# A hybrid RWKV and attention block on one core: other tiles' work on VectorE queued behind the inverse, chunk-local products in pairs of groups

## The chip, the core and the metric

The kernel runs on one core of a Trainium2 chip. A core has five engines with instruction queues of their own: TensorE (matmuls; PE in the profile, PEld its weight loads), VectorE (DVE), ScalarE (ACT), GpSimd (POOL) and SyncE (SP, here only a queue of DMA issues). Each works through its queue in order and waits for semaphores of the others. The metric is the device time of one execution, in microseconds; lower is better.

## The reference

One layer over 512 positions of width 2048, batch 1, all in float32. The RWKV branch and the attention branch share one normalised input, and their gated sum goes through an output projection.

```python
def hybrid_layer(x, ...):
    h = rms_norm(x, norm_g)
    proj = jnp.einsum('btd,de->bte', h, w_in)
    shifted = centred_shift(proj[..., :SHIFT_WIDTH], shift_mu)
    xr, xk, xv, wdown, adown = _split(shifted, SHIFT_SIZES)
    z_r, q, k, v, z_a, gates = _split(proj[..., SHIFT_WIDTH:], REST_SIZES)
    o_r = rwkv7_bidir(xr, xk, xv, wdown, adown, ...) * jax.nn.silu(z_r)
    o_a = axial_gqa(q, k, v, q_norm_g, k_norm_g) * jax.nn.silu(z_a)
    p_r = jnp.einsum('btc,cd->btd', o_r, w_branch_rwkv)
    p_a = jnp.einsum('btc,cd->btd', o_a, w_branch_attn)
    merged = sigmoid(g_r) * p_r + sigmoid(g_a) * p_a
    return x + jnp.einsum('btd,de->bte', merged, w_out)

def _wkv_step(S, inp):          # rwkv7_bidir scans this over time, in both directions
    w, kk, b, k, v, r = inp
    sa = jnp.einsum('dbhvk,dbhk->dbhv', S, -kk)
    S = S * w[..., None, :] + sa[..., None] * b[..., None, :] + v[..., :, None] * k[..., None, :]
    return S, jnp.einsum('dbhvk,dbhk->dbhv', S, r)
```

`rwkv7_bidir` has 16 heads of 64 channels. Behind the scan come a group norm over each head's channels, scale and bias, and a term `coef * v`. A final RMS norm ends the reference.

## The kernel before, in words

Every large product is split in a high and a low float32r part, and is made as three matmuls of 128x512 ("dense" work, line 291, tile `acc`). The weights come in quarter strips (`raw` by DMA on SP, high part `wh` on ACT, low part `wl` on DVE, line 265; twelve matmuls each).

The RWKV branch is worked in eight tiles of 128 channels (two heads), each in chunks of 64 positions. A tile passes through these steps:

- `stage_a(i)`: rates and decays. It loads `la` (SP, 1 MB), maps it (L504, DVE), normalises `kk` (`pss`, `rs`, `rb`, `prb`), and for both directions makes a running sum (L517, a scan on DVE; L522 its correction), exponentials (ACT, L530 to L532), and the products `BK` (L538, DVE) with help from POOL. Temporaries come from a ring `temp` of four buffers.
- `tile_task(i)`: products `AL` (DVE, L556 to L559), then chunk-local products `lr` (L571, TensorE) in four visits, each of one group of two chunks; each visit writes two PSUM banks, which DVE (L574 to L578) and ACT (L573) empty. Then `pv`, and the inverse of the chunks' triangular matrices on DVE: 30 steps of L607 and L608, and transposes and copies that end with L625 (`XB`). On TensorE the transposes `tb` (L633) and a product `pcf` (L637, L638) follow the `lr` visits. Flag `B` is set there; the task then waits `subwait`, 50000 ns of the planner's time, and goes on with `pq` (L645) and `px` (L653), which need the inverse.
- The chain over chunks, eight times: `pa` (L678), ACT copies `a0s` and others (L680 to L683), `pu` (L693), ACT copies, `px2` (L700), and the new state `SV` on DVE (L706, four pieces), which the next `pa` needs. POOL prepares `SV` and `sd` (L673, L689).
- `stage_e(i)`: group norm (L722 to L730 on DVE, a square on ACT, a power on POOL), transposes `pg` (L736), two products (L742, L743), and a store to DRAM on POOL's queue. `sz` is loaded on SP's queue.

PSUM has eight banks: two for `acc`, a ring of three named "g" (`g_tile`) and a ring of three named "c" (`c_tile`, used by the chain).

The order on TensorE in this part is the order in which the program issues it. `Weave` is a planner at build time: tasks are generators which yield (cost, wait, flag needed), in ns; while no task is due, it issues one dense matmul and counts `UNIT` for it. The order on the other engines is worked out by the scheduler of the tile framework from its own estimated times. Strips `k`, `r` and `v` of a tile wait for flag B of the tile before. The rest of the input projection (60 strips) fills in. Behind the RWKV part come the attention stage (64 units, with what is left of the input strips, and then the products of the RWKV branch from `oq` as filler; there TensorE's order too is the scheduler's), the products of the attention branch, and the output projection.

Of the kernel before, what the change touches and what calls it, by code (L numbers as in the profile page):

```python
# [100 lines left out]
class Weave:  # L101
# [3 lines left out]

    UNIT = 217
    LAG = 100
# [105 lines left out]

OPT = dict(manual=True, tls=True, sub="dve", subwait=50000, fwait=6000, gn=15000, u1=0, u2=0, c1=700, c2=700, c3=1150, fly=3, scale='pool', prb=4, low=1300, warm=24, rwt='tile', every=2, auto=1, man=1)

# [9 lines left out]
def emit_all(nc, tc, A, out, dbg):  # L225
# [252 lines left out]

    fact = {}

    def stage_a(i):
# [21 lines left out]
        ve.tensor_copy(rb, rs[:, 8:16].rearrange("p (t h) -> p t h", h=2).unsqueeze(3).to_broadcast([128, 4, 2, C]))  # L503
        ve.tensor_scalar(out=la, in0=la, scalar1=0.5, scalar2=0.5, op0=ALU.mult, op1=ALU.add)  # L504
        yield 250, 4500, None
        prb = g_tile("prb")
        for tt in range(4):
            pe.transpose(prb[:, tt * 128:(tt + 1) * 128], rb[:, tt].rearrange("p h c -> p (h c)"), ident)
        ve.tensor_tensor(out=kk, in0=kk, in1=prb, op=ALU.mult)
        ks = rw.tile([128, T], F32, name="ks", bufs=2)  # L510
        dirs = []
# [31 lines left out]
        W.flag(f"A{i}", 6000)  # L543
        yield 428, 0, None

    def tile_task(i):
# [16 lines left out]
        for c in range(0, NC, 2):  # L563
            two = slice(c, c + 2)

            lr = [g_tile("lr").rearrange("p (d c t) -> p d c t", d=2, c=2) for _ in range(2)]
            for d in range(2):
                for j in range(2):
                    for eo in range(2):
                        h0 = 64 * eo  # L570
                        pe.matmul(lr[eo][:, d, j, :], lhsT=BK[h0:h0 + 64, d, c + j, :], rhs=AL[h0:h0 + 64, d, c + j, eo, :], start=True, stop=True)  # L571
            m2 = lambda rows, eo, c0_, c1_: mk[rows, :, eo, c0_:c1_].unsqueeze(2).to_broadcast([64, 2, 2, c1_ - c0_])
            ac.copy(LB[lo_, :, two, :], lr[0][lo_, :, :, 0:C])  # L573
            ve.tensor_tensor(out=AL[hi_, :, two, 0, :], in0=lr[0][hi_], in1=m2(hi_, 0, 0, 128), op=ALU.mult)  # L574
            ve.tensor_tensor(out=L2[lo_, :, two, 0, C:128], in0=lr[0][lo_, :, :, C:128], in1=m2(lo_, 0, C, 128), op=ALU.mult)
            ac.copy(LB[hi_, :, two, :], lr[1][hi_, :, :, C:128])
            ve.tensor_tensor(out=AL[lo_, :, two, 1, :], in0=lr[1][lo_], in1=m2(lo_, 1, 0, 128), op=ALU.mult)
            ve.tensor_tensor(out=L2[hi_, :, two, 1, 0:C], in0=lr[1][hi_, :, :, 0:C], in1=m2(hi_, 1, 0, C), op=ALU.mult)  # L578
            yield 900, 2300, None
        pv = g_tile("pv")  # L580
# [42 lines left out]
        for q in range(4):  # L623
            rows = slice(q * 32, q * 32 + 32)
            ve.tensor_copy(XB[rows], XT[1 - q % 2][rows, 1 - q % 2])  # L625
            for d in range(2):
                ac.copy(XP[rows, d, :, q * 32:(q + 1) * 32], XT[d][rows, d])

        for d in range(2):
            for g in range(2):  # L630
                tb = g_tile("tb").rearrange("p (c h t) -> p c h t", c=4, h=2)
                for j in range(4):
# [6 lines left out]
        ve.tensor_tensor(out=ks, in0=pcf, in1=v, op=ALU.mult)  # L639
        W.flag(f"B{i}")  # L640
        yield 432, OPT['subwait'], None

# [19 lines left out]
        for n in range(NC):  # L662
# [22 lines left out]
            if n < NC - 1:  # L685
                for d in range(2):
                    for eo in range(2):
                        h = slice(64 * eo, 64 * eo + 64)
                        po.tensor_scalar(out=sd[h, d, eo, :], in0=SV[h, d, eo, 0, :], scalar1=PC[h, d, cc[d]:cc[d] + 1], scalar2=0.0, op0=ALU.mult, op1=ALU.add)  # L689
            yield 450, OPT['c1'], None  # L690
            pu = c_tile("pu").rearrange("p (d x) -> p d x", d=8)
# [20 lines left out]
        ve.tensor_tensor(out=O[:, 0], in0=O[:, 0], in1=O[:, 1], op=ALU.add)  # L712
        ow = ch(temp("ow"))
        ve.tensor_tensor(out=ow, in0=O[:, 0, 0:NC, :], in1=O[:, 0, NC:2 * NC, :], op=ALU.add)
        W.flag(f"D{i}")
        W.add(2, stage_e(i, ow, ks))
        yield 450, 0, None

    def stage_e(i, ow, ks):

        s8 = rw.tile([128, 32], F32, name="s8")
        ve.tensor_reduce(out=s8[:, 0:8], in_=ow, axis=AX.X, op=ALU.add)  # L722
        ve.tensor_scalar(out=s8[:, 8:16], in0=s8[:, 0:8], scalar1=-1.0 / C, scalar2=None, op0=ALU.mult)
# [6 lines left out]
        ve.tensor_tensor(out=ow, in0=ow, in1=s8[:, 24:32].unsqueeze(2).to_broadcast([128, NC, C]), op=ALU.mult)  # L730
        gc = temp("gc")
        yield 0, OPT['gn'], None
        for g in range(2):
            pg = g_tile("pg").rearrange("p (c e t) -> p c e t", c=4, e=2)
            for j in range(4):
                pe.transpose(pg[0:64, j].rearrange("p e t -> p (e t)"), ow[:, 4 * g + j, :], ident)  # L736
            for eo, h0 in ((1, 0), (0, 64)):
                ac.copy(ch(gc)[h0:h0 + 64, 4 * g:4 * g + 4, :], pg[0:64, :, eo, :])
            yield 428, 0, None
        sz = rw.tile([128, T], F32, name="sz", tag="sz")  # L740
        sp.dma_start(out=sz, in_=fsp[i])
        ve.scalar_tensor_tensor(out=gc, in0=gc, scalar=pc(P_GW + i), in1=ks, op0=ALU.mult, op1=ALU.add)  # L742
        ve.scalar_tensor_tensor(out=gc, in0=gc, scalar=pc(P_GB + i), in1=sz, op0=ALU.add, op1=ALU.mult)  # L743
        po.dma_start(out=osp[i], in_=gc)
        tap(f"og{i}", gc)

    W.flag("ad", 4500)
# [344 lines left out]
```

## Time and the profile before

| What | us |
|---|---|
| median of 3 runs | 1792.86 (1791.39 to 1794.54) |
| the profiled execution's own time | 1792.16 |
| its span | 1789.9 |
| TensorE busy | 1717.1 (96%) |
| DVE busy | 1221.1 (68%) |
| ACT busy | 812.6 (45%) |
| POOL busy | 554.0 (31%) |

The time of an execution is a little longer than the span from its first to its last instruction. Busy time counts an engine's instructions from start to end. A wait is put down to the engine whose semaphore came last. The granted clock is that of TensorE, as a share of 2.4 GHz.

### The profile page before, as it was taken

Reading aid. Unit: us, or ns where it says so; the run is one execution under the profiler, and the core shown is the slowest. Engines: PE = TensorE matmul, PEld = TensorE weight load, DVE = VectorE, ACT = ScalarE, POOL = GpSimd, SP = SyncE. Lnnn points to the kernel's source line nnn. Section 1 sums busy time; section 2 is a strip of 40 time slices with the busy share of each in tenths; the row PEclk is TensorE's granted clock in tenths of the full one; section 3 lists DMA queues with packets and bytes.
Section 4 is the critical chain, followed back from the end, with each engine's and each line's share of the span. In section 5 each row is a group of like instructions: output and inputs, shape, how many; then the busy total and the mean of one; then the engine's idle time right before and its main releaser. Section 6 shows DMA issues by size and latency. Waiting matters only on the chain. (4 is left out here: it accounts for less than half of the span.)

```text
span 1789.9 us, 26075 instructions
## 1 busy us (share of the span) xinstructions
PE 1717.1 (96%) x8972; PEld 1431.3 (80%) x8972; DVE 1221.1 (68%) x2360; ACT 812.6 (45%) x1827; POOL 554.0 (31%) x824
## 2 busy tenths in 40 slices
PE   6999999999999999999999999999989998999997
PEld 6877887887887887887887888888768886788876
DVE  6577859759959948967957957923788887443342
ACT  5544354354354444344344344344566666232231
POOL 3131062053153143053053043022555554331110
PEclk9999999999999999999999999999999999999999
DMA  6564323423323322423323322433443320435452
GB/s 219 167 201 122 106 63 111 108 60 98 103 77 104 104 63 92 111 74 100 106 77 95 105 67 82 116 89 108 149 149 104 99 92 26 143 108 154 130 171 106
DMA packets 96851, 194.87 MB, mean 109 GB/s; under 512 B 11088, under 2 KB 11344, under 8 KB 95312
## 3 DMA queue, kind: packets, MB, share of 16 engines
q1 hardware_dynamic: 77616, 152.18, 29.7%
q10 hardware_dynamic: 15264, 28.46, 4.4%
q0 software_dynamic: 3840, 12.59, 2.4%
q8 instruction: 71, 1.16, 0.3%
q14 instruction: 60, 0.49, 0.1%
HBM read 162.77 MB, written 30.41 MB: 108 GB/s over the span
## 5 line engine op out<-in xcount | busy, mean ns | idle before, releaser
L291 PE MATMUL acc<-hh,wl 128*128 128x512 f32 (+1 forms) x1388 | 552.1, 398 | 5.1 <-DVE wl L265 5.1
L291 PE MATMUL acc<-hh,wh 128*128 128x512 f32 (+1 forms) x1388 | 554.2, 399 | 0.6 <-ACT wh L264 0.6
L291 PE MATMUL acc<-hl,wh 128*128 128x512 f32 (+1 forms) x1388 | 551.3, 397 | 2.8 <-DVE hl L386 2.2
L265 DVE TENSOR_TENSOR wl<-raw,wh 128x512 fp32r<-128x512 f32 x445 | 331.9, 748 | 278.7 <-ACT wh L264 268.3
L264 ACT CAST wh<-raw 128x512 fp32r<-128x512 f32 x472 | 292.3, 620 | 499.9 <-PE acc L291 348.3
L291 PEld LDWEIGHTS acc<-hh,wl 128*128 128x128 f32 x1388 | 263.2, 190 | 57.5 <-DVE wl L265 8.2
L291 PEld LDWEIGHTS acc<-hl,wh 128*128 128x128 f32 x1388 | 263.4, 190 | 53.1 <-DVE hl L386 4.2
L291 PEld LDWEIGHTS acc<-hh,wh 128*128 128x128 f32 x1388 | 263.4, 190 | 51.5 <-ACT wh L264 1.7
L673 POOL TENSOR_SCALAR SV<-VT 64x128 f32<-64x128 f32 x256 | 82.2, 321 | 214.3 <-PE px L700 110.1
L706 DVE SCALAR_TENSOR_TENSOR SV<-px,PC,sd 64x64 f32<-64x64 f32 x224 | 63.5, 283 | 79.6 <-PE px L700 73.3
L689 POOL TENSOR_SCALAR sd<-SV,PC 64x64 f32<-64x64 f32 x224 | 89.5, 400 | 17.4
L291 PE MATMUL acc<-oq,wh 128*128 128x512 f32 x256 | 84.1, 400 | 4.0 <-ACT oq L946 4.0
L607 DVE TENSOR_TENSOR tm<-B 128x30 f32<-128x30 f32 (+14 forms) x240 | 82.3, 343 | 6.1
L608 DVE TENSOR_TENSOR B<-B,tm 128x30 f32<-128x30 f32 (+14 forms) x240 | 81.1, 338 | 6.0
L527 POOL TENSOR_TENSOR ks<-ks,k 128x512 f32<-128x512 f32 x8 | 15.2, 1901 | 223.4 <-ACT wh L264 84.0
L1023 PE MATMUL of<-wl,mh 128*128 128x512 f32 x192 | 75.0, 391 | 1.8 <-DVE wl L265 1.8
L678 PEld LDWEIGHTS pa<-SV,AL 128*128 128x128 f32 x512 | 67.3, 191 | 10.2 <-POOL SV L673 2.3
L1024 PE MATMUL of<-wh,ml 128*128 128x512 f32 x192 | 74.7, 389 | 0.0
L700 PEld LDWEIGHTS px<-SV,L 128*128 128x128 f32 x512 | 67.9, 193 | 7.3 <-ACT SV L694 1.8
L678 PE MATMUL pa<-SV,AL 128*128 128x64 f32 x512 | 67.2, 271 | 3.3 <-DVE SV L706 3.3
L1022 PE MATMUL of<-wh,mh 128*128 128x512 f32 x192 | 66.1, 389 | 0.0
L700 PE MATMUL px<-SV,L 128*128 128x64 f32 x512 | 65.6, 271 | 0.0
(688 smaller groups left out, 2879.4 us busy)
## 6 DMA issues: line engine op xcount, KB each, us to landing
raw<-in_w_in_dram SPq DMA_DIRECT2D x344, 256.0 KB, 3.1
raw<-in_wo_dram SPq DMA_DIRECT2D x64, 256.0 KB, 2.8
fsp<-tg ACTq DMA_DIRECT2D x60, 256.0 KB, 2.5
tsp<-la ACTq DMA_DIRECT2D x32, 256.0 KB, 3.4
la<-tsp SPq DMA_DIRECT2D x8, 1024.0 KB, 5.0
raw<-in_wbr_dram SPq DMA_DIRECT2D x32, 256.0 KB, 3.1
tgm<-fsp POOLq DMA_DIRECT2D x32, 256.0 KB, 3.5
raw<-in_wba_dram SPq DMA_DIRECT2D x32, 256.0 KB, 2.9
```

The costliest lines, as they stand in the source:

```text
L264: ac.copy(dst_hi, src)
L265: (eng or ve).tensor_tensor(out=dst_lo, in0=src, in1=f(dst_hi), op=ALU.subtract)
L291: pe.matmul(acc[:, tok], lhsT=w[1 if u == 2 else 0][:, j, :], rhs=(xl if u == 1 else xh)[:, kt, tok], start=(kt == 0 and u == 0 and tok.st ...
L607: se.tensor_tensor(out=tv, in0=B[:, 0:s, s:s + 1].to_broadcast([128, s, n]), in1=B[:, s:s + 1, s + 1:32].to_broadcast([128, s, n]), op=ALU ...
L608: se.tensor_tensor(out=B[:, 0:s, s + 1:32], in0=B[:, 0:s, s + 1:32], in1=tv, op=ALU.add)
L673: po.tensor_scalar(out=SV[v0:v0 + 64, d, eo], in0=src.unsqueeze(1).to_broadcast([64, 2, C]), scalar1=1.0, scalar2=0.0, op0=ALU.mult, op1=A ...
L678: pe.matmul(pa[:, d, eo, :], lhsT=AL[:, d, cc[d], eo, :], rhs=SV[:, d, eo, 0, :], start=True, stop=True)
L689: po.tensor_scalar(out=sd[h, d, eo, :], in0=SV[h, d, eo, 0, :], scalar1=PC[h, d, cc[d]:cc[d] + 1], scalar2=0.0, op0=ALU.mult, op1=ALU.add)
L700: pe.matmul(px2[:, d, eo, :], lhsT=L2[:, d, cc[d], eo, :], rhs=SV[:, d, eo, 1, :], start=True, stop=True)
L1022: pe.matmul(acc, lhsT=mh[:, dt, tok(tt)], rhs=w[0], start=(dt == 0), stop=False)
L1023: pe.matmul(acc, lhsT=mh[:, dt, tok(tt)], rhs=w[1], start=False, stop=False)
L1024: pe.matmul(acc, lhsT=ml[:, dt, tok(tt)], rhs=w[0], start=False, stop=(dt == NKT - 1))
```

## The change

`UNIT` goes from 217 to 227 and `subwait` from 50000 to 45500. A helper `behind(i)` puts the instructions of a block, on their engine, behind the last copy of tile i's inverse. The mapping of `la` in `stage_a(i)` is put behind the inverse of tile i-1, and the first group norm instruction of tile i behind the inverse of tile i+1, for which the task also waits for a flag X, set 3000 ns before `subwait` ends. `stage_a` from the third tile on waits for the end of an older tile's group norm (flag E) before it takes `ks`; the output `ow` has a buffer of its own, `sz` takes one of the ring, and its load is issued before `pg`. The `lr` products go two groups a visit, one of the two banks of a group from each ring; `tb` alternates between the rings. The first chunk waits 1600 ns longer between `pa` and `pu`.

```diff
-    UNIT = 217
+    UNIT = 227
-OPT = dict(... subwait=50000, ...)
+OPT = dict(... subwait=45500, ...)
+    fact, inv = {}, {}
+    def behind(i):
+        return tc.issue_after(inv[i].ins) if i in inv else nullcontext()
 def stage_a(i):
-        ve.tensor_scalar(out=la, in0=la, scalar1=0.5, scalar2=0.5, op0=ALU.mult, op1=ALU.add)
+        with behind(i - 1):
+            ve.tensor_scalar(out=la, in0=la, scalar1=0.5, scalar2=0.5, op0=ALU.mult, op1=ALU.add)
...
         ve.tensor_tensor(out=kk, in0=kk, in1=prb, op=ALU.mult)
+        if i >= 2:
+            yield 428, 0, f"E{i - 2}"
...
-        yield 428, 0, None
+        yield 0 if i >= 2 else 428, 0, None
 def tile_task(i):
-            lr = [g_tile("lr").rearrange(...) for _ in range(2)]
+            lr = [t_("lr").rearrange(...) for t_ in (g_tile, c_tile)]
...
-            yield 900, 2300, None
+            if c == 2:
+                yield 1800, 5000, None
+        yield 1800, 3000, None
...
-            ve.tensor_copy(XB[rows], XT[1 - q % 2][rows, 1 - q % 2])
+            inv[i] = ve.tensor_copy(XB[rows], XT[1 - q % 2][rows, 1 - q % 2])
...
-                tb = g_tile("tb").rearrange(...)
+                tb = (g_tile if g else c_tile)("tb").rearrange(...)
...
         W.flag(f"B{i}")
+        W.flag(f"X{i}", OPT['subwait'] - 3000)
...
-            yield 450, OPT['c1'], None
+            yield 450, OPT['c1'] + (1600 if n == 0 else 0), None
...
-        ow = ch(temp("ow"))
+        if i:
+            yield 450, 0, f"E{i - 1}"
+        ow = ch(rw.tile([128, T], F32, name="ow", tag="ow"))
...
-        yield 450, 0, None
+        yield 0 if i else 450, 0, None
 def stage_e(i, ow, ks):
+        if i < NT - 1:
+            yield 0, 0, f"X{i + 1}"
-        ve.tensor_reduce(out=s8[:, 0:8], in_=ow, axis=AX.X, op=ALU.add)
+        with behind(i + 1):
+            ve.tensor_reduce(out=s8[:, 0:8], in_=ow, axis=AX.X, op=ALU.add)
...
-        gc = temp("gc")
         yield 0, OPT['gn'], None
+        gc, sz = temp("gc"), temp("sz")
+        sp.dma_start(out=sz, in_=fsp[i])
         for g in range(2):
...
-            yield 428, 0, None
-        sz = rw.tile([128, T], F32, name="sz", tag="sz")
-        sp.dma_start(out=sz, in_=fsp[i])
...
         po.dma_start(out=osp[i], in_=gc)
+        W.flag(f"E{i}")
+        yield 856, 0, None
```

## Rows read from the trace of the kernel before

**Rows 1.** The page, busy time: us, share of the span, instructions.

```profile
PE 1717.1 (96%) x8972; PEld 1431.3 (80%) x8972; DVE 1221.1 (68%) x2360; ACT 812.6 (45%) x1827; POOL 554.0 (31%) x824
```

**Rows 2.** Waits of TensorE, 140 to 1250: waited for, total, times, longest.

```profile
PE lr L571 <- DVE s L728: 9.6, 3, 3.7
PE pu L693 <- ACT a0s L681: 5.8, 10, 3.1
PE lr L571 <- DVE L L575: 4.4, 3, 2.1
PE tb L633 <- ACT VT L584: 3.6, 5, 0.7
PE pa L678 <- DVE SV L706: 3.3, 5, 1.9
```

**Rows 3.** Timeline of TensorE, third tile, second `lr` visit: start, length, what.

```profile
421.76 1.13 PE L571 MATMUL lr<-AL,BK 64*128 64x128 f32 x14 [2.97 <-DVE s L728]
...
423.83 0.63 PE L291 MATMUL acc<-hh,wl 128*128 128x512 f32 x1
424.26 0.63 PE L291 MATMUL acc<-hh,wh 128*128 128x512 f32 x1
```

**Rows 4.** Timeline of DVE, the same stretch.

```profile
413.30 1.22 DVE L504 TENSOR_SCALAR la<-la 128x2048 f32<-128x2048 f32 x1
414.44 0.68 DVE L722 TENSOR_REDUCE s<-ow 128x8 f32<-128x512 f32 x1
...
415.63 1.22 DVE L517 TENSOR_TENSOR_SCAN cs<-con,la 128x512 f32<-128x512 f32 x1
...
417.49 0.69 DVE L724 TENSOR_TENSOR ow<-ow,s 128x512 f32<-128x512 f32 x1
...
420.49 0.69 DVE L574 TENSOR_TENSOR AL<-lr,con 64x512 f32<-64x512 f32 x1
```

**Rows 5.** Timeline of TensorE around one undisturbed `lr` visit.

```profile
287.39 0.39 PE L291 MATMUL acc<-hl,wh 128*128 128x512 f32 x1
287.71 1.16 PE L571 MATMUL lr<-AL,BK 64*128 64x128 f32 x16
288.80 0.50 PE L291 MATMUL acc<-hh,wl 128*128 128x512 f32 x1
289.14 0.39 PE L291 MATMUL acc<-hh,wh 128*128 128x512 f32 x1
289.37 0.40 PE L291 MATMUL acc<-hl,wh 128*128 128x512 f32 x1
```

**Rows 6.** Stretches: length, busy us of each engine, granted clock, DMA.

```profile
420.00:440.00 20.00, 17.47 (x109) 14.13 (x110) 16.27 (x33) 10.63 (x23) 6.25 (x12) 0.91 0.28 80
635.00:655.00 20.00, 16.95 (x89) 14.67 (x88) 7.63 (x16) 9.91 (x31) 5.23 (x16) 0.83 0.22 63
695.00:715.00 20.00, 17.23 (x102) 13.87 (x103) 15.24 (x30) 9.08 (x21) 5.42 (x9) 0.83 0.26 79
...
1515.00:1540.00 25.00, 20.17 (x69) 15.29 (x70) 10.37 (x16) 6.79 (x12) 10.43 (x11) 0.80 0.39 124
```

**Rows 7.** Timelines of DVE and TensorE, fourth tile: the inverse ends, `pq` starts.

```profile
617.28 0.59 DVE L625 COPY XX<-RR 32x256 f32<-32x256 f32 x2
...
628.43 0.42 PE L645 MATMUL pq<-XX,LQ 128*128 128x32 f32 x3
```

**Rows 8.** Stretches behind the second tile's inverse; columns PE, PEld, DVE, ACT, POOL.

```profile
343.00:357.00 14.00, 14.00 (x70) 11.82 (x68) 7.26 (x13) 4.97 (x9) 0.09 (x1) 1.00 0.43 104
356.00:375.00 19.00, 17.74 (x116) 15.26 (x115) 15.96 (x21) 10.50 (x29) 13.24 (x12) 1.00 0.19 55
```

**Rows 9.** Line L538 on DVE: ns min/median/max, first and last start.

```profile
L538 DVE TENSOR_TENSOR BK<-ke,la x16: 683/1664/1782, 113.8 to 1046.8; 64x512 f32<-64x512 f32 x16
```

**Rows 10.** Waits of TensorE, 1250 to 1530.

```profile
PE acc L291 <- ACT oq L946: 4.0, 1, 4.0
PE acc L291 <- ACT oah L264: 3.4, 1, 3.4
PE acc L291 <- DVE tgm L988: 2.3, 1, 2.3
```

More of the change, by code (lines that the diff above doesn't have):

```diff
@@ L211, in step @@
         return True
-OPT = dict(manual=True, tls=True, sub="dve", subwait=50000, fwait=6000, gn=15000, u1=0, u2=0, c1=700, c2=700, c3=1150, fly=3, scale='pool', prb=4, low=1300, warm=24, rwt='tile', every=2, auto=1, man=1)
+OPT = dict(manual=True, tls=True, sub="dve", subwait=45500, fwait=6000, gn=15000, u1=0, u2=0, c1=700, c2=700, c3=1150, fly=3, scale='pool', prb=4, low=1300, warm=24, rwt='tile', every=2, auto=1, man=1)
 def context(nc):
@@ L477, in filler @@
         strip(s, done)
-    fact = {}
+    fact, inv = {}, {}
+    def behind(i):
+        return tc.issue_after(inv[i].ins) if i in inv else nullcontext()
     def stage_a(i):
@@ L564, in tile_task @@
             two = slice(c, c + 2)
-            lr = [g_tile("lr").rearrange("p (d c t) -> p d c t", d=2, c=2) for _ in range(2)]
+            lr = [t_("lr").rearrange("p (d c t) -> p d c t", d=2, c=2) for t_ in (g_tile, c_tile)]
             for d in range(2):
@@ L630, in tile_task @@
             for g in range(2):
-                tb = g_tile("tb").rearrange("p (c h t) -> p c h t", c=4, h=2)
+                tb = (g_tile if g else c_tile)("tb").rearrange("p (c h t) -> p c h t", c=4, h=2)
                 for j in range(4):
```

## The prediction

> **What bounds the kernel now.** I read the share of busy time first. TensorE is busy for 1717.1 us of a span of 1789.9 [rows 1], so the end is set by the matmul queue, and a gain can come only from the 73 us in which that queue stands still, from the time in which it runs at a lower granted clock, and from gaps between matmuls. The second view is therefore the list of TensorE's waits between 140 and 1250 us, where the eight RWKV tiles are worked [rows 2]. The chunk-local products `lr` (L571) wait 9.6 us for DVE's L728 and 4.4 us for DVE's L575; the transposes `tb` (L633) wait 3.6 us; `pu` (L693) waits 5.8 us for ACT's `a0s`; `pa` (L678) waits 3.3 us for DVE's `SV`. None of these is a wait for data of the weights. L728 is group norm of the tile before, and has nothing to do with `lr`.
>
> The third view, the timelines of both engines, shows why. The third tile's second `lr` visit stops after two matmuls and stands 2.97 us [rows 3]. It needs the PSUM bank of the first visit, and DVE empties that bank only from 420.49 us on [rows 4], because the rates of the next tile (1.22 us), its scan (1.22), and group norm (0.68 and 0.69 shown, two like them and two small ones not shown) stand ahead of it in DVE's queue. After the stall the dense matmuls come 0.43 us apart [rows 3] and not 0.23 [rows 5]: the granted clock has fallen to the lower of its two levels, 1.2 GHz. The fourth view gives that a price: mean granted clock by stretch [rows 6]. A mean of 0.91 over 20 us is 1.8 us of lost matmul time, 0.83 is 3.4, and 0.80 over 25 us is 5.0.
>
> The planner's fill is not lost when a wait is shortened. Dense matmuls that no longer stand inside a tile are issued later, so I count stalls, clock and gaps, and not the shorter waits themselves.
>
> **What the change removes from `lr`.** The pieces of rows 4 that stand ahead of the bank's emptying are all queued behind a tile's inverse, and the two `lr` banks now come from two rings of three, so that a visit of two groups takes four banks of six. The second visit begins 23 dense matmuls later (5000/227, rounded up), 23 x 0.23 = 5.3 us; its second group alone reuses banks, and reaches them after its first group, 1.09 us [rows 5], 6.4 us after the first visit. Emptying one group costs DVE about 2.2 us (0.69 for one of two large pieces in rows 4, and two of half the columns), so it is done in time even with two weight pieces of 0.68 between. The 14.0 us of `lr` waits in rows 2 go. `tb` wants a bank right behind `pv`; its first bank now comes from the other ring and has been free for a visit, so the 3.6 us go as well. Sum 17.6; bounds 0 to 17.6; I take 17, since the timelines name the pieces one by one.
>
> **Fewer visits.** Into a visit the step is 0.32 us where dense matmuls are 0.23 apart, out of it 0.34 [rows 5]: 0.09 + 0.11 = 0.2 us a visit. Two visits instead of four, eight tiles: 16 x 0.2 = 3.2 us. Nothing in the rows excludes that as small a gap appears elsewhere: bounds 0 to 3.2, I take 3.2.
>
> **The shorter wait for the inverse** (`subwait`, and `UNIT`). Before it is 50000/217, 231 dense matmuls; after it is 45500/227, 201. That is 30 x 0.23 = 6.9 us earlier for `pq`. The inverse of the fourth tile ends at 617.87 us and `pq` starts at 628.43 [rows 7]: 10.6 us of slack, of which 3.7 stay. So the cost is nothing, hidden under dense work; if the inverse came later by more than 3.7 us, each us more would be one us for each of eight tiles. It should not come later: what is now emptied in two groups (4.4 us) was before held up by group norm.
>
> **What is moved, and where it lands.** Rates, first scan, and group norm now start when the inverse ends, some 4 us ahead of `pq`. In that stretch today DVE is busy 7.26 of 14 us and POOL 0.09 [rows 8]. The moved pieces by rows 4 are 1.22 + 1.22 + four of 0.69 or so, 4 us, plus the correction of the scan (0.7) and the products with `gc` (2 us): about 6.7 us. They don't fit whole into the 3.7 us that are left. Behind it lies the stretch 356 to 375, in which DVE is already busy 15.96 of 19 us [rows 8] with the products `BK`, and the chain over chunks starts there: each chunk needs a `SV` product from DVE (four pieces, 1.2 us together) with only six dense matmuls, 1.4 us, to cover it. What is queued behind DVE's `SV` is `pa` of the next chunk on TensorE's queue, in order, and all dense work behind that. So the saturated stretch grows from two chunks to about four. Today `pa` loses 3.3 us [rows 2] over some 14 such chunks, 0.24 each; 28 of them at the same rate lose 6.7, and I take 7.3, a cost of 4 us. Bounds: a gain of 3.3 (if the order within DVE falls well) and a loss of 43 (28 times 1.66, the median of the slow `BK` pieces of rows 9, less today's 3.3).
>
> What could make the moved pieces dearer is POOL. One kind of `BK` product takes 683 ns at best and 1664 in the median, in one shape [rows 9], and in the stretch 356 to 375 POOL is busy 13.24 of 19 us [rows 8]. If the four moved pieces with two inputs slip past `pq` and stretch as these do, each costs 1.0 us more (1.66 - 0.69); ahead of `pq`, where POOL idles, nothing. The Trainium skill, "SBUF — State Buffer", section "Who interferes with whom", says that a VectorE instruction with two SBUF inputs contends with a GpSimd instruction that reads SBUF, and that one blocks the other for the whole instruction; the trace's two durations agree. By that rule 4 us of DVE a tile are at risk and by the row of the idle stretch none; it is the mechanism of the first rival below.
>
> The other moves. The load of `sz` (SP) and the store of `gc` (POOL) go with group norm; SP's queue stands ahead of TensorE by three quarter strips of weights, and the waits of rows 2 name no weight piece, so both cost nothing; if that cover were gone, a load would show as `acc` waiting for `wl`. Waits for E (a tile's group norm ended) before `ks` and `ow`: by the planner's constants the group norm of the tile before ends 42.5 + 15 us behind the B mark, and the chain only starts at 45.5, with eight chunks to go, so nothing waits. What these waits hold up is a task of the planner, not an engine.
>
> **`pu` of the first chunk** has 1600 ns more cover, 7 dense matmuls, 1.6 us. Of the 5.8 us in rows 2 the longest was 3.1, which it halves; ACT gets exponentials of the moved scan there too. I take a gain of 4 (bounds 0 and 5.8).
>
> **The clock.** The dips at 420 and 695 us (1.8 and 3.4) follow `lr` stalls and go with them; the one at 635 (3.4) follows the longest `pu` wait. That is 8.6; I put one dip of 1.8 back for the longer `SV` waits: gain 6.8, bounds 0 and 8.6.
>
> **The attention stage.** Per tile the planner places fewer dense matmuls: 30 (`subwait`), 7 (`lr`: 44 before, 37 after), one before `lr`, less 7 (first chunk): 31 x 8 = 248, 57 us of work that moves behind the eighth tile. Today the attention stage runs out of such work: TensorE waits 3.4 us for the last head and 2.3 for a gate at its end [rows 10], and loses 5.0 to the clock there [rows 6]. With 57 us more in hand these 10.7 can be covered. But the wait for `oq`, 4.0 us [rows 10], which follows the last `w_in` strip, moves into the middle of attention and may grow. Bounds: gain 10.7, loss 4; I take a gain of 7.
>
> **The sum**, against the profiled execution's own 1792.2 us (0.7 below the median of the runs, a difference I neglect): -17 - 3.2 - 4 + 4 - 6.8 - 7 = -34.0, so 1758 us.
>
> **Rivals.** (1) The moved pieces slip past `pq` and stretch beside POOL, 4 us of DVE a tile, so the crowding is worse than today's rate: each of the 28 `SV` pieces is 0.6 us late, 17 us instead of 7.3, with three more dips of 1.8: 10 + 5.4 = 15 us back, 1773. For it: DVE has 3 us free in 19 already. Against: today's 0.24. (2) The other side: each `SV` waits behind one whole `BK` piece of 1.66 us, 46 us, 43 more than today, and every tile but the last has a dip, 10.8 beyond the one counted. Without its 4 us for `SV` the sum is -38; -38 + 43 + 10.8 = +16, 1808. The point from which it decides is (38 - 10.8 + 3.3)/28, about 1.1 us of lateness per `SV`. Against: the queue's order is written down beforehand from estimated durations, and today's order loses a quarter of that. (3) The inverse is late for `pq`: 6 us later than today is 2.3 us on eight tiles, 18 us, with a dip each 14: 32 back, 1790, no change. For it: a remaining slack of 3.7 us. Against: what was ahead of it is taken away.
>
> **How the numbers follow.** The forecast, with 1743 (every bound in favour: 17.6 + 3.2 + 5.8 + 3.3 + 8.6 + 10.7 = 49.2) to 1768 as its own range, 0.62. Rival 1, 0.20. Rival 2, 0.09. Rival 3, 0.05. The remaining 0.04 is below 1743: short waits and dips that the rows shown leave out. The range of 8 in 10 reaches from 1739 to 1784. A measurement of this kernel tells 0.2% from no change. Faster by more than that, 0.85; within, 0.06; slower, 0.09.
>
> **What would show it.** Right: in the list of TensorE's waits `lr` and `tb` all but vanish; a tile has two `lr` visits of 32; DVE's L504, L722 and L724 stand behind L625; dense work from `oq` is left after the last head, and the dips at 420, 635 and 695 have no successors. Wrong: `pa` waiting for L706 far beyond 7 us, `pq` waiting for L622, `acc` waiting for `wl`, or a new wait of `pg` for group norm.

## The result, and the profile after

The changed kernel takes 1802.50 us (median of 7 runs, 1797.59 to 1808.81), the kernel before 1791.39 beside it on the same chip (1789.84 to 1794.54). The ratio is 1.0062, 95% interval 1.0040 to 1.0083: slower by 0.6%, where 1.9% faster was forecast. The span of the profiled execution is 1802.9 us, 13.0 more than before.

The busy times of the page after, to be held beside [rows 1]:

```profile
PE 1730.0 (96%) x8972; PEld 1454.1 (81%) x8972; DVE 1209.8 (67%) x2358; ACT 813.4 (45%) x1827; POOL 572.3 (32%) x826
```

TensorE has as many instructions as before and is busy 12.9 us longer. That is all but 0.1 us of the longer span; so the time in which TensorE stands still is the same in sum, and it has only changed its place. Two stretches by windows say where, of the kernel before and then of the one after (length, busy time of PE, PEld, DVE, ACT, POOL, granted clock, DMA share, GB/s):

```profile
140.00:1200.00 1060.00, 1030.08 (x5621) 862.63 (x5621) 799.80 (x1595) 468.80 (x1156) 310.12 (x569) 0.99 0.33 93
1200.00:1600.00 400.00, 385.55 (x1984) 321.37 (x1983) 267.33 (x527) 212.31 (x436) 184.57 (x201) 0.98 0.36 110
```

```profile
140.00:1200.00 1060.00, 1017.66 (x5520) 861.46 (x5519) 786.37 (x1599) 463.37 (x1171) 330.29 (x595) 0.95 0.30 87
1200.00:1600.00 400.00, 394.54 (x2011) 330.43 (x2010) 262.78 (x512) 210.71 (x406) 177.29 (x173) 1.00 0.39 119
```

In the RWKV part TensorE stood still for 1060 - 1030.1 = 29.9 us and now for 42.3, and the granted clock fell from 0.99 to 0.95. In the attention part it stood still for 14.5 and now for 5.5, and the clock rose to 1.00. The second row is the gain that was forecast there; the first is the loss. Its waits by name, TensorE between 140 and 1250 us of the kernel after (total, times, longest):

```profile
PE pa L688 <- DVE SV L716: 16.2, 11, 3.0
PE px L710 <- ACT SV L704: 12.0, 5, 2.5
PE pu L703 <- ACT a0s L691: 5.8, 8, 1.1
PE px L663 <- ACT LQ L659: 5.5, 4, 2.8
PE pss L502 <- ACT sq L497: 2.5, 1, 2.5
```

Against [rows 2], every wait of `lr` and `tb` is gone, as forecast. In their place stand the links of the chain over chunks: `pa` for the state `SV`, 16.2 us for 3.3, and two waits that were not in the list before, of both products named `px` for ACT's copies, 17.5 together. (L688, L703 and L710 are L678, L693 and L700 of the code shown above, L663 is L653, and L659 makes its `LQ`; L545 below is L538, L716 is L706, L704 and L705 are the copies of `pu` into `SV`, L513 is `prb`.)

What such a wait looks like: the fifth tile's chain, third and fourth chunk. First TensorE, then ACT, then DVE of the kernel after (start, length, what, idle time before it and its releaser):

```profile
764.14 0.66 PE L703 MATMUL pu<-a0s,XP 128*128 128x64 f32 x4 [0.91 <-ACT a0s L691]
...
768.14 1.97 PE L710 MATMUL px<-SV,L 128*128 128x64 f32 x8 [2.36 <-ACT SV L704]
769.87 0.77 PE L291 MATMUL acc<-hh,wh 128*128 128x512 f32 x1
770.45 0.63 PE L291 MATMUL acc<-hl,wh 128*128 128x512 f32 x1
770.87 0.63 PE L291 MATMUL acc<-hh,wl 128*128 128x512 f32 x1
...
773.69 1.94 PE L688 MATMUL pa<-SV,AL 128*128 128x64 f32 x8 [0.91 <-DVE SV L716]
```

```profile
766.79 0.63 ACT L538 ACTIVATE cs<-cs 128x512 f32<-128x512 f32 x1 [2.27 <-POOL la L526]
767.33 0.61 ACT L539 ACTIVATE la<-la 128x512 f32<-128x512 f32 x1
767.85 0.24 ACT L704 COPY SV<-pu 64x128 f32<-64x128 f32 x1
```

```profile
761.40 1.23 DVE L524 TENSOR_TENSOR_SCAN cs<-con,la 128x512 f32<-128x512 f32 x1
...
768.37 4.87 DVE L545 TENSOR_TENSOR BK<-ke,la 64x512 f32<-64x512 f32 x2 [1.32 <-POOL ke L534]
773.27 1.23 DVE L716 SCALAR_TENSOR_TENSOR SV<-px,PC,sd 64x64 f32<-64x64 f32 x4
```

`pu` is done by 764.8, and two copies on ACT, of 0.24 and 0.26 us, are all that `px` then needs. They stand in ACT's queue behind two exponentials of the next tile's rates, and the first of these waits 2.27 us for POOL. So TensorE waits 2.36 us for ACT, and its dense matmuls, in the same queue behind `px`, with it. Then DVE's `SV` stands behind two pieces of `BK` that take 4.87 us, and `pa` waits again. From the first of the two stalls on the dense matmuls come 0.43 us apart; the granted clock of the next 8 us is 0.50 (the stretches 762 to 770 and 770 to 778 of the kernel after):

```profile
762.00:770.00 8.00, 4.74 (x26) 3.78 (x25) 6.22 (x7) 4.01 (x13) 7.64 (x10) 0.86 0.07 21
770.00:778.00 8.00, 7.09 (x24) 5.63 (x23) 7.74 (x12) 2.08 (x7) 7.32 (x11) 0.50 0.11 38
```

Scan, exponentials, `BK` and `ks` of the next tile, here the "rates", lie in the middle of the chain over chunks. How far in they lie is the number on which the experiments turned. From the timelines of TensorE and DVE, as a mean over the second to seventh tile, in us behind `pcf`:

| kernel | `prb` | first `pa` | `BK` begins | `BK` ends | its end behind the first `pa` |
|---|---|---|---|---|---|
| before | 53.4 | 58.7 | 53.9 | 64.2 | 5.5 |
| after | 60.8 | 53.2 | 73.7 | 84.7 | 31.5 |

### The profile page after: what moved, and what is told of

It reads as the page before. It is cut to its first block, busy times and chain, and to the rows that moved or that the text cites. A ratio compares the mean times of both kernels' runs of the same rounds, so it can differ in the third digit from the quotient of the medians.

```text
span 1802.9 us, 26064 instructions
## 1 busy us (share of the span) xinstructions
PE 1730.0 (96%) x8972; PEld 1454.1 (81%) x8972; DVE 1209.8 (67%) x2358; ACT 813.4 (45%) x1827; POOL 572.3 (32%) x826
## 3 DMA queue, kind: packets, MB, share of 16 engines
q1 hardware_dynamic: 77616, 152.18, 29.1%
## 4 chain that ended last, share of the span: by engine, by line
PE 49%; DVE 4%; issue 1%; ACT 1%; POOL 1%; DMA 1%; POOLq 0%; DVEq 0%
PE acc L291 31%; PE of L1038 2%; PE of L1039 2%; PE of L1037 2%; PE po L929 2%; PE pT L914 1%; PE px L710 1%; PE pa L688 1%; PE sc L897 1%; PE sc L898 1%; DVE wl L265 1%; PE lr L578 1%; PE pu L703 1%; PE acc L1039 1%; PE acc L1037 1%
## 5 line engine op out<-in xcount | busy, mean ns | idle before, releaser
L291 PE MATMUL acc<-hh,wl 128*128 128x512 f32 (+1 forms) x1388 | 558.9, 403 | 5.3 <-DVE wl L265 5.3
L291 PE MATMUL acc<-hh,wh 128*128 128x512 f32 (+1 forms) x1388 | 561.0, 404 | 0.0
L291 PE MATMUL acc<-hl,wh 128*128 128x512 f32 (+1 forms) x1388 | 558.0, 402 | 2.6 <-DVE hl L386 2.3
L265 DVE TENSOR_TENSOR wl<-raw,wh 128x512 fp32r<-128x512 f32 x443 | 327.1, 741 | 254.4 <-ACT wh L264 242.5
L699 POOL TENSOR_SCALAR sd<-SV,PC 64x64 f32<-64x64 f32 x224 | 110.4, 494 | 18.4 <-DVE SV L716 0.8
L716 DVE SCALAR_TENSOR_TENSOR SV<-px,PC,sd 64x64 f32<-64x64 f32 x224 | 63.4, 283 | 64.5 <-PE px L710 58.7
L530 POOL TENSOR_TENSOR la<-cs,la 128x512 f32<-128x512 f32 x8 | 12.9, 1609 | 290.3 <-DVE cs L529 290.3
L688 PEld LDWEIGHTS pa<-SV,AL 128*128 128x128 f32 x512 | 74.5, 212 | 24.3 <-issue 10.8
L710 PEld LDWEIGHTS px<-SV,L 128*128 128x128 f32 x512 | 73.7, 209 | 21.5 <-ACT SV L704 16.0
L688 PE MATMUL pa<-SV,AL 128*128 128x64 f32 x512 | 74.9, 293 | 16.2 <-DVE SV L716 16.2
L710 PE MATMUL px<-SV,L 128*128 128x64 f32 x512 | 71.9, 288 | 12.0 <-ACT SV L704 12.0
```

Source lines behind the costliest of these rows:

```text
L265: (eng or ve).tensor_tensor(out=dst_lo, in0=src, in1=f(dst_hi), op=ALU.subtract)
L291: pe.matmul(acc[:, tok], lhsT=w[1 if u == 2 else 0][:, j, :], rhs=(xl if u == 1 else xh)[:, kt, tok], start=(kt == 0 and u == 0 and tok.st ...
L688: pe.matmul(pa[:, d, eo, :], lhsT=AL[:, d, cc[d], eo, :], rhs=SV[:, d, eo, 0, :], start=True, stop=True)
L710: pe.matmul(px2[:, d, eo, :], lhsT=L2[:, d, cc[d], eo, :], rhs=SV[:, d, eo, 1, :], start=True, stop=True)
```

## The experiments

Theories at the start: **A**, the shorter wait for the inverse is what costs; **B**, the pieces queued behind the inverse are; **C**, which came later, the two delays add up, and taking back one leaves the other. Each kernel below is timed against the kernel before on its own chip (medians there 1789.98 to 1791.24). Ratios have their 95% interval; "waits" are TensorE's, 140 to 1250 us, all names summed.

**The wait as long as before.** The chain again begins 231 dense matmuls behind `pcf`, and flag X keeps its time.

```diff
-        W.flag(f"X{i}", OPT['subwait'] - 3000)
-        yield 432, OPT['subwait'], None
+        W.flag(f"X{i}", 42500)
+        yield 432, 52400, None
```

> Two theories of the loss. (A) The shorter wait: the changed kernel starts pq after 201 dense matmuls, but the strips k, r, v of the next tile need about 212 behind flag B, so its rates (from pss on) start after the chain and fall on chunks 2 to 4, where they delay SV and the copies of ACT. (B) The moved pieces: rates and group norm placed behind the inverse crowd the chain wherever it starts. Here only the wait goes back to 231 dense matmuls; the X mark stays where it was. A: waits of pa, px and pu fall from 39.5 us to about 10, slow clock in the RWKV stage from 102 us to about 30, and the time is about 1765 us. B: waits stay above 25 us, and the time is 1795 or more.

1795.13 us, 1.0026 [1.0015, 1.0037], waits 40.7 of which `pa` for `SV` 29.8. Only 7 us better than the change, as theory B had it and not A (1765).

**The rates free.** `la` is not queued behind the inverse (`with behind(i - 1)` becomes `if True`).

> The changed kernel without the order behind the inverse for la (so the second direction's scan and exponentials can run in the lr stretch as before); group norm stays behind. A: the chain still starts ahead of pss, the products BK still fall on chunks 2 to 4: waits above 30 us, 1797 or more. B with the rates as the heavy part: chain waits fall below 20 us, and the time is 1785 or less.

1786.19 us, 0.9974 [0.9959, 0.9988], waits 37.5 (`pa` 18.8, `px` for ACT's `SV` 11.9). That is neither theory's: A had 1797 or more, B waits below 20.

**Group norm free.** The task doesn't wait for X, and its first instruction isn't queued behind the next inverse.

```diff
-        if i < NT - 1:
-            yield 0, 0, f"X{i + 1}"
-        with behind(i + 1):
+        if True:
```

> The changed kernel with group norm right behind the chain as before (no X wait, no order behind the inverse); the rates stay behind. This also sets flag E early, so the rest of stage_a waits for nothing. A: chain waits fall only a little, 30 us or more, 1795 or more. B with group norm, or the E wait, as the heavy part: below 20 us, and 1785 or less.

1795.29 us, 1.0029 [1.0017, 1.0041], waits 40.6 (`pa` 19.8, `px` L663 for ACT's `LQ` 12.6). That is where A had it, and B was wrong for group norm at the short wait. No single part, taken back alone, takes back the loss.

**Pairs of groups and two rings alone**, put into the kernel before.

```diff
-            lr = [g_tile("lr").rearrange(...) for _ in range(2)]
+            lr = [t_("lr").rearrange(...) for t_ in (g_tile, c_tile)]
...
-            yield 900, 2300, None
+            if c == 2:
+                yield 1800, 4900, None
+        yield 1800, 3000, None
...
-                tb = g_tile("tb").rearrange(...)
+                tb = (g_tile if g else c_tile)("tb").rearrange(...)
```

> The kernel before with the lr products two groups a visit and the banks from two rings (tb too), and nothing else. Both theories: no new waits in the chain, since order and start are those of before. The lr and tb waits of 20 us fall to about 8, because the second visit stands 5.5 us and not 2.5 behind the first, though group norm and rates still stand ahead on DVE; with 3 us or more from fewer visits and some clock, about 1772 us. If visits in pairs themselves cost (A and B both wrong), slower than 1791.

1779.83 us, 0.9939 [0.9921, 0.9957]. No wait of `lr` or `tb` is left, with group norm and rates where they always were; `pg` waits instead, 16.4 us; 1772 was expected. **The same with `pg` later** (`gn=30000`) and 1600 ns more cover for the first `pu`:

> pairs_only with group norm's transposes pg 30 us and not 15 behind the chain, so that they meet neither the lr visits nor an unfinished group norm, and with 1600 ns more for the first chunk's pu; nothing is placed behind the inverse. If the 16 us of pg waits in pairs_only are a matter of when pg stands in TensorE's order, they go, pu falls to about 1 us, and the time is about 1762 us. If they come back as lr or tb waits, 1778.

1773.03 us, 0.9900 [0.9883, 0.9917], waits 20.9; 1762 was expected, but no wait of `pg` is left. So the part of the change that removes the `lr` stalls brings 0.6% by itself and 1.0% with these two edits, and the rest of the change takes more than that away.

**Group norm's release earlier** in the change (X at 34000 in place of 42500), with the short wait, and with the long one (52400):

> Theory A alone (the shorter wait) and theory B alone (the moved pieces) have fallen. Theory C: two delays add up. The chain starts 30 dense matmuls earlier, and the second half of stage_a, which is issued only behind flag E, comes later because E lies behind group norm's pg at X + 15 us; each puts the products BK behind the first SV pieces, and taking back one leaves the other. Here the X mark alone moves from 42500 to 34000, so E comes 8.5 us earlier; the chain starts early as in the change. C: waits of the chain stay near 30 us, 1785 to 1797. If E alone is the cause: waits under 15 us and 1770 or less.

> X at 34000 and the chain at 231 dense matmuls again: both delays are taken back, with rates and group norm still behind the inverse. C: the products BK all stand ahead of the first SV on DVE, chain waits fall below 12 us, slow clock in the RWKV stage below 35 us, and the time is 1760 to 1775. B (the moved pieces themselves crowd the chain): waits above 25 us and 1790.

1803.71 us, 1.0072 [1.0052, 1.0093], waits 49.9; and 1790.34 us, 0.9990 [0.9976, 1.0003], waits 38.8. The earlier release is worth nothing with the short wait and 4.8 us with the long one. In the second `pa` waits only 5.7, but `px` waits 15.8 for ACT's copies. Theory C missed both times: it had 1785 to 1797 and 1760 to 1775.

**Group norm free and the long wait**, both edits above together:

> Group norm right behind the chain as before (E early), rates behind the inverse, and the chain at 231 dense matmuls. C: chain waits below 12 us, with some 2 to 5 us of waits at pg, 1765 to 1778. B with the rates: above 25 us and 1790.

1772.24 us, 0.9890 [0.9869, 0.9911], waits 25.6. The time is as theory C had it, the waits are not (below 12). Three kernels fill in a table by which the delays do not add. **Nothing behind an inverse, short wait; the same, long wait; and that with `gn=22000`**:

> The changed kernel with nothing queued behind an inverse (rates and group norm both where they were), and the short wait of 201 dense matmuls kept. It prices the short wait with no piece moved. Theory D (the short wait hurts only through pieces that it leaves too little room): about 1775 (1768 to 1780), waits in the RWKV part about 28 us. Theory A again (the wait is short by itself: the v strip and the products that follow it are late for the chain): 1785 to 1795, as with group norm alone set free (1795), and the waits 35 to 40, of px for ACT and pa for DVE.

> The same with the wait of 231 dense matmuls: pairs of groups, two rings, the longer cover of the first pu, and nothing moved. If the rates' move behind the inverse still costs something when group norm is free and the wait long, this is some 3 to 8 us under 1772, because the wait of prb for DVE's rb (5.6 us) goes, but lr may wait for DVE's la again (2 to 4 us). If the rates' move is good by itself it is 3 to 8 us above. My guess is 1770.

> The same, with the transposes pg of group norm 7000 ns of planner's time later (22000 for 15000), so that they don't meet the lr visits. The wait of pg for DVE (3 us) goes, and the next rates' second half, which waits for flag E, is a little later: 1768 to 1772. It is the best guess at a version that beats both kernels; 1780 or more would say that a delay of 7 us of the rates' second half already hurts.

1793.93 us, 1.0020 [1.0005, 1.0034]; 1773.37 us, 0.9911 [0.9885, 0.9938]; 1772.33 us, 0.9902 [0.9882, 0.9922].

| queued behind the inverse | wait 201 dense | wait 231 dense |
|---|---|---|
| rates and group norm | 1802.5 (the change) | 1795.1 |
| group norm | 1786.2 | not run |
| rates | 1795.3 | 1772.2 |
| nothing | 1793.9 | 1773.4 |

The short wait by itself costs 20.6 us (1793.9 - 1773.4), the two moves by themselves 21.7 (1795.1 - 1773.4), and all of it 29.1 (1802.5 - 1773.4): less than the sum, so theory C is wrong in that the delays add. The rates' move by itself costs 1 us or nothing at either wait. Group norm behind the inverse costs 22.9 us on top of the rates' move at the long wait (1795.1 - 1772.2) and 7.2 at the short one. Without the rates' move it was run at the short wait only, and there it is 7.7 us faster than nothing moved (1786.2 for 1793.9): 15.7 us of waits of `pg` for group norm are not there. So what it costs without the rates' move at the long wait is not known.

The price of the short wait is what remains after a gain. Between 1200 and 1600 us TensorE stands still for 5.4 to 6.4 us in the five kernels with the short wait, and for 12.7 us or more in all the others.

The waits of the two kernels with nothing moved, short and then long:

```profile
PE pa L688 <- DVE SV L716: 26.9, 11, 4.8
PE pg L750 <- DVE ow L743: 8.7, 5, 2.8
```

```profile
PE pg L750 <- DVE ow L743: 9.7, 6, 2.2
PE pa L688 <- DVE SV L716: 9.7, 4, 3.9
```

The two profiled executions are 17.5 us apart, and `pa` waits 17.2 us longer for `SV` in the first. In the timelines the first `pa` stands 52.0 us behind `pcf` in the one and 58.7 in the other, and `prb`, on which the rates depend through `kk`, 57.7 and 53.9. `prb` comes behind the strips of weights that make `k`, `r` and `v` (`stage_a` waits for all three), and these are dense matmuls: with 30 of them taken from ahead of the chain, the rates are late for it. So theory A is right of the short wait, and the expectation's other theory, that the wait hurts only through pieces that were moved, falls: unmoved rates are late too.

That gave **theory D**: whatever delays the next tile's rates, or brings the chain forward, sets them among the chunks, where one long wait on an engine that works in order blocks `SV`. Its rival **E**: group norm's own work is too much in that stretch. A first attempt was to hold back the rates in the 1772.2 us kernel by a flag of the planner:

```diff
-            yield 428, 0, f"E{i - 2}"
+            yield 0, 0, f"E{i - 2}"; yield 428, 0, f"X{i - 1}"
...
-        W.flag(f"X{i}", 42500)
+        W.flag(f"X{i}", 58400)
```

> The kernel that ran at 1772.2 us (group norm where it was before, 231 dense matmuls in the wait for the inverse), with one thing put back: the second half of the rates of the next tile (scan, exponentials, the BK products) may be issued no earlier than in the changed kernel with the longer wait (58400 ns of planner's time behind the product pcf), though group norm itself stays early. Theory D (what hurts is that the rates are late, whoever delays them): it loses most of the 23 us again, 1788 to 1796, TensorE's waits in the RWKV part rise from 25 to about 40 us with pa waiting for DVE's SV some 25, and BK stands among the SV of the first chunks. Theory E (what hurts is group norm's own work on DVE and ACT among the chunks): it stays within 5 us of 1772, with pa waiting 10 to 14.

1772.07 us, 0.9891 [0.9872, 0.9909], waits 25.4. It tells nothing for E: TensorE's order is the same as without the edit, and `BK` ends 6.8 us behind the first `pa`, where it was 7.1. The flag held nothing back. The next kernel forces it: **the scans queued behind the second chunk's `SV`**.

```diff
-            yield 428, 0, f"E{i - 2}"
+            yield 428, 0, f"S{i - 1}"
...
-            ve.tensor_tensor_scan(cs, rst, sg, 0.0, ALU.mult, ALU.add)
+            with behind((i - 1, 's')): ve.tensor_tensor_scan(cs, rst, sg, 0.0, ALU.mult, ALU.add)
...
-                        ve.scalar_tensor_tensor(out=SN[h, d, eo, 0, :], ...)
+                        last = ve.scalar_tensor_tensor(out=SN[h, d, eo, 0, :], ...)
                 SV = SN
+                if n == 1: W.flag(f"S{i}"); inv[i, 's'] = last
```

> The 1772 us kernel (group norm free, long wait) with one piece forced late: from the third tile on, the scans of the next tile's rates are queued on DVE behind the second chunk's SV, so that exponentials, BK and ks fall among the third to sixth chunk, as they do in the changed kernel. Group norm, the wait for the inverse and TensorE's dense work stay. Theory D (a chain of the rates that lands among the chunks is what blocks SV on the engines that work in order): most of the loss comes back, 1786 to 1796, waits in the RWKV part 38 to 48 us for 25, of pa for DVE's SV and px for ACT's SV. Theory F (the place of BK is a symptom; what counts is how much dense work stands between pq and the chain): 1770 to 1776.

1792.46 us, 1.0003 [0.9991, 1.0016]: 20 us of the gain are lost by this one delay, with group norm early and the long wait, as theory D had it. Waits 41.4, and their first row; then DVE's timeline at one of the stalls:

```profile
PE pa L688 <- DVE SV L716: 31.6, 7, 5.7
```

```profile
924.14 2.94 DVE L545 TENSOR_TENSOR BK<-la,cs 64x512 f32<-64x512 f32 x2 [2.26 <-ACT cs L538]
927.10 2.35 DVE L545 TENSOR_TENSOR BK<-ks,cs 64x512 f32<-64x512 f32 x2
929.48 1.23 DVE L716 SCALAR_TENSOR_TENSOR SV<-px,PC,sd 64x64 f32<-64x64 f32 x4
```

`px`, which `SV` needs, ran at 921.63 for 1.00 us. `SV` starts 6.8 us later, behind a `BK` that itself waited for an exponential. Five tiles lose 5.3 to 5.7 us each at this one place. Theory F, by which the dense work between `pq` and the chain counts and the place of `BK` does not, falls: the first `pa` stands 58.7 us behind `pcf`, as in the kernel before, and TensorE's order is that of the 1772.2 us kernel.

**One block taken away.** The kernel with X at 34000 and the long wait (1790.3 us) has three waits of `px` of 4.6 to 5.4 us. One of them on TensorE, with ACT's and DVE's queues at that time:

```profile
506.23 1.97 PE L710 MATMUL px<-SV,L 128*128 128x64 f32 x8 [5.43 <-ACT SV L704]
```

```profile
504.88 0.62 ACT L264 CAST ch__5316<-ks 128x512 fp32r<-128x512 f32 x1 [6.45 <-DVE ks L548]
505.41 0.61 ACT L264 CAST wh<-raw 128x512 fp32r<-128x512 f32 x1
505.93 0.25 ACT L704 COPY SV<-pu 64x128 f32<-64x128 f32 x1
```

```profile
501.71 2.36 DVE L545 TENSOR_TENSOR BK<-la,cs 64x512 f32<-64x512 f32 x2
504.10 0.75 DVE L548 SCALAR_TENSOR_TENSOR ks<-r,par,ks 128x512 f32<-128x512 f32 x1
```

A cast of `ks`, wanted only for the next `pcf`, stands ahead of the copies. It goes behind the copies of the last chunk, and with it POOL's subtraction (`cl_`), which reads it:

```diff
-            ac.copy(SV[64:128, :, 1, 1, :], pu[64:128, 0:2, :])
+            inv[i, 'c'] = ac.copy(SV[64:128, :, 1, 1, :], pu[64:128, 0:2, :])
...
-        split(ch_, cl_, ks, po)
+        with behind((i - 1, 'c')):
+            split(ch_, cl_, ks, po)
```

> The kernel with group norm queued behind the inverse, flag X early and the wait of 231 dense matmuls (1790.3 us). Its waits are mostly three of 4.6 to 5.4 us of px for ACT's SV copies, and in each ACT's cast of ks (wanted only at pcf, 50 us later) stands ahead of the copies and waits 4.7 to 6.5 us for DVE's ks, the end of the rates. Here that cast is queued behind the SV copies of the same tile's last chunk, and nothing else is changed. Theory D: the 15.8 us of px for SV go, all but 1 or 2, with the dips that follow them, 1770 to 1778: then group norm behind the inverse costs nothing by itself. Theory E (group norm's work is too much there): another instruction takes the cast's place, waits stay at 33 to 39 us, and the time at 1785 to 1792.

1778.33 us, 0.9939 [0.9918, 0.9960], 12 us faster by the place of one cast of 0.62 us a tile and of what reads it; 0.3 us above theory D's range. Its waits:

```profile
PE pa L689 <- DVE SV L717: 14.2, 8, 3.0
PE pss L502 <- ACT sq L497: 5.1, 2, 2.7
PE pg L753 <- DVE ow L746: 4.8, 4, 1.8
```

`px` no longer waits for the copies (15.8 us gone), but `pa` waits 8.5 us more than it did. Theory E falls in the main: of the 22.9 us that group norm behind the inverse cost on top of the rates' move, 4.8 go with the earlier X (1795.1 to 1790.3), 12.0 with the cast, and 6.1 are left above the 1772.2 us kernel. Theory D had nothing left there; how much of those is group norm's own work stays open.

The end of `BK` behind the first `pa`, and the waits, over all kernels of the experiments but the one whose flag held nothing back:

| kernel | `BK` ends behind first `pa` | waits | us |
|---|---|---|---|
| nothing moved, long wait | 6.2 | 28.9 | 1773.4 |
| the same, `gn=22000` | 6.8 | 20.6 | 1772.3 |
| group norm free, long wait | 7.1 | 25.6 | 1772.2 |
| pairs, `pg` later | 8.0 | 20.9 | 1773.0 |
| pairs alone | 8.3 | 28.6 | 1779.8 |
| cast behind | 9.3 | 29.8 | 1778.3 |
| X at 34000, long wait | 9.5 | 38.8 | 1790.3 |
| nothing moved, short wait | 17.6 | 46.8 | 1793.9 |
| both moved, long wait | 18.4 | 40.7 | 1795.1 |
| group norm free, short wait | 20.3 | 40.6 | 1795.3 |
| X at 34000, short wait | 24.3 | 49.9 | 1803.7 |
| scans forced late | 30.1 | 41.4 | 1792.5 |
| rates free, short wait | 31.0 | 37.5 | 1786.2 |
| the change | 31.5 | 42.4 | 1802.5 |

Up to some 10 us the rates do little harm, unless something on ACT waits for their end; with 17 or more all kernels have 37 us of waits or more. Among these the time doesn't follow the lateness any further. The five kernels at 1772.1 to 1773.4 us are 0.9 to 1.1% faster than before and can't be told apart. Why the rates freed alone (1786.2) are so much better than the change at the same place of `BK` is not settled; its waits are 5 us shorter, and its mean granted clock from 140 to 1200 us is 0.97 for 0.95. Most of that lies 75 to 90 us behind `pcf`, where TensorE stands still about as long (12.7 and 13.0 us over the second to seventh tile) at a mean clock of 0.76 for 0.65.

## Why the prediction was wrong, step by step

**`lr` and `tb`, forecast -17: right**, and by the two rings and pairs more than by the moves, as the kernel with these alone shows: it has no such wait either. The forecast put the gain down to both together; the moves were not needed for these waits, but without them `pg` waits for group norm, until it is put later.

**Fewer visits, -3.2: right in kind.** TensorE's idle time ahead of the `lr` products for which the profile names no releaser (us, times), before and after:

```profile
  issue: 11.0, 32
```

```profile
  issue: 4.9, 14
```

It falls by 6.1 us. Some of the before may be slow clock.

**The shorter wait, forecast 0: this step failed.** "So the cost is nothing, hidden under dense work" looked at one operand only, the inverse, and there it was right: no wait for its copies appears, they end 5.3 to 10.4 us ahead of `pq` in the eight tiles, and rival 3 is out. What the step left out is that the dense matmuls in the wait are the strips from which the next tile's `k`, `r` and `v` are made. With nothing moved, taking 30 away sets `prb` from 4.8 us ahead of the first `pa` to 5.7 behind, and that costs 20.6 us.

**What is moved, forecast +4: this step failed too.** The moves cost 21.7 us at the long wait and 8.6 on top of the short one (1802.5 - 1793.9). The step spread the lateness evenly, 0.24 us over 28 `SV` pieces. In the trace it comes as single waits of up to 3.0 us (5.8 at the long wait), because not the length of the moved pieces counts, but the chain behind them (scan, POOL, exponentials, `BK`, `ks`, cast), each link of which waits at the head of another engine's queue: the kernel with the scans forced late does the same work as the one at 1772.2 and loses 20 us. Group norm behind the inverse costs 22.9 us on top of the rates' move at the long wait. The step said that E would not make the rates wait, since it counted planner's time up to the end of group norm; but `ks` has two buffers, the new one needs that which L755 of group norm reads, and L755 comes after `pg`, which is then among the chunks (760.45 us in the tile shown, 12 us behind its first `pa`). And it looked at DVE only; 25.8 of the 42.4 us are waits for ACT, 17.5 of them the new ones of `px`.

The moved pieces with two inputs were not the dearer for POOL: the two of group norm (L739, L745) took at most 0.69 us, the two products with `gc` 0.75 and 0.80. `BK` is another matter. One of the four kinds of `BK` in the kernel after, in one shape (ns min/median/max):

```profile
L545 DVE TENSOR_TENSOR BK<-ke,la x16: 689/1228/3119, 110.6 to 1042.6; 64x512 f32<-64x512 f32 x16
```

In [rows 9] the longest was 1782, now 3119, though the median fell from 1664 to 1228 and the sum over all four kinds hardly changed (62.7 us before, 63.4 after); where the pair above took 4.87 us, POOL is busy for 7.64 and 7.32 of 8 us. The Trainium skill, "SBUF — State Buffer", section "Who interferes with whom", says that a VectorE instruction with two SBUF inputs contends with a GpSimd instruction that reads SBUF; the durations agree with it, and no run here took POOL's part away.

**`pu`, forecast -4: 0.** The total is 5.8 as before, but the longest fell from 3.1 to 1.1. With nothing else in its way it works: 0.6 with nothing moved and the long wait.

**The clock, forecast -6.8: wrong in sign.** The dips of [rows 6] are there to compare. The tiles run earlier in the kernel after, so the first, second and fourth row are the stretches that lie as far from `pcf` of their tile as 420, 635 and 695 do in the kernel before; the last row is the second half of the attention part:

```profile
404.00:424.00 20.00, 20.00 (x142) 16.59 (x141) 16.77 (x34) 8.58 (x18) 1.91 (x7) 1.00 0.27 83
619.00:639.00 20.00, 16.36 (x94) 13.72 (x93) 12.00 (x21) 9.85 (x29) 13.18 (x22) 0.89 0.22 62
635.00:655.00 20.00, 17.73 (x78) 15.24 (x79) 14.55 (x21) 7.65 (x24) 15.74 (x24) 0.67 0.15 40
673.00:693.00 20.00, 20.00 (x140) 16.59 (x139) 16.89 (x31) 7.72 (x17) 1.14 (x5) 1.00 0.40 122
1400.00:1600.00 200.00, 200.00 (x1014) 167.58 (x1013) 123.26 (x242) 92.81 (x179) 80.65 (x86) 1.00 0.37 115
```

The dips of the `lr` stalls (420, 695) and of the tail (1515) are gone. The one in the chain (635) is 0.89 for 0.83 at its place, but right behind it, at 635 of the kernel after, there is one of 0.67, and one like it in other tiles, as at 770 above. At that place the kernel before has full clock:

```profile
651.00:671.00 20.00, 20.00 (x125) 17.55 (x125) 6.89 (x18) 10.40 (x37) 9.21 (x29) 1.00 0.25 70
```

Visits and clock together were to take 10 us off TensorE's busy time. With nothing moved and the long wait it is 14.9 us less (1702.2 for 1717.1), so this term holds where neither of the two steps above is taken. In the change it grew by 12.9, and this is 23 us of the 47 that lie between the forecast and the measurement in span (-34 and +13.0). The stalls make 29: the forecast has -17 in the RWKV part, the windows +12.4. (Some 5 us go the other way: 2 more than forecast in the attention part, and 3 ahead of 140 us.)

**The attention part, -7: right.** Idle time there fell by 9.0 us, and the waits for `oq`, `oah` and the gate of [rows 10] are down to a fraction; one for a weight piece, `acc` for `wl`, grew from 1.7 to 3.6 us. The gain hangs on the short wait, as the forecast had it: no kernel with the long wait has it.

**The rivals.** Rival 2 came closest, 1808 for 1802.5, and named the place: `SV` behind whole `BK` pieces. It got 0.09 because today's rate of lateness seemed to speak against it; that rate came from a trace in which `BK` ends before the second chunk (in five of the six tiles of the table), and said nothing of one where it does not. Its form was off: not 46 us of `pa`, but 16.2 and as much again on ACT, and the clock.

## What to carry to other kernels

A wait that is filled with other work is shortened at the price of everything that the filler was making: list what depends on it, not only what the wait was for. When work moves into a chain that runs link by link over several engines, price it by the longest block that it can put at the head of each engine's queue in order, ACT and POOL too, and not by a mean rate taken where that block was absent. Two edits that each delay the same thing need not add (here 20.6 and 21.7 us alone, 29.1 together), so a part is cleared only by a run in which the other is undone as well.

## What the runs showed of the hardware

A stall of 2.36 us on TensorE was followed by some 8 us at a granted clock of 0.50 with dense matmuls 0.43 us apart, and these cost more than the stall: of the 30.9 us of span between the change and the kernel with group norm free and the long wait (1802.9 and 1772.0), 23.0 are TensorE's busy time (1730.0 and 1707.0), at the same 8972 instructions. A `BK` product that takes 689 ns at best took up to 3119 ns in one shape. And one cast of 0.62 us a tile, put with what reads it at another place in its engine's queue, was worth 12 us of 1790.
